# An encoder layer as a stream of weight tiles: one more buffer for classical tiles, seven products in one more projection block, and quarter sums of the residual made in another place

## The chip, the cores and the metric

The kernel runs on one core of a Trainium2 chip. The metric is the device time of one execution in microseconds (us), the median of several runs. Before the change it is 1144.56 us (three runs, 1144.2 to 1146.13).

The core's engines each run their own instruction stream: PE (matrix products; its weight loads are listed apart as PEld), DVE (vector), ACT (scalar, with its tables), POOL (GpSimd) and SP, which here only issues loads. Transfers run on 16 DMA engines that all queues of the core share. Products accumulate in eight PSUM banks of 128 x 512 floats.

## The reference

One layer of a transformer encoder on 256 positions of 2048 features, in float32:

```
n     = rmsnorm(x)
q_a, k_a, v_a, q_r, k_r, v_r, g_r = split(n @ W_in)      # 2048 x 7168
A     = attention of 8 heads (three dilated windows, ALiBi), softmax
R     = retention of 8 heads in both directions, normed per head, times silu(g_r)
h     = x + concat(A, R) @ W_out                          # 2048 x 2048
y     = rmsnorm(h + (silu(rmsnorm(h) @ W_gate) * (rmsnorm(h) @ W_up)) @ W_down)   # 5632 wide
```

Nearly all of the work is in the weight products, and the weights (some 220 MB) are read once.

## The kernel before, in words

**Precision.** A float32 product is made of three products of a shorter format: high by high, low by high, high by low. So each operand exists as a pair of halves. `halved` (L164) makes them: ACT copies the high half (its instructions carry L156, the line of the helper `copy`), then DVE subtracts it from the source for the low half (L159, the helper `tt`). A weight tile of 128 x 1024 floats (512 KB) thus costs one load on SP's queue, one ACT and one DVE instruction before PE can use it. In the profile the loaded tile is `rawc_...`, `raw_...` or `rawt_...`, its halves `ws_...`, the products' banks `p_...`.

**Blocks.** The weights are worked off in blocks of 1024 output columns in two sections: seven of the input projection (in0 to in6; pairs of q, k, v, g sections), two of the output projection (o0, o1), then three groups of gate-and-up blocks (gu0 to gu10) each followed by two down blocks. `ORDERS` writes the order of each block's steps out by hand. A step C is a classical weight tile: 12 matmuls into four banks. The steps 1a to 7a (and 1b to 7b) are the seven products of a Winograd scheme that replaces four classical tiles: 6 matmuls each, 42 in place of 48. Products 1, 2 and 4 read the activations themselves, 3, 5, 6 and 7 read quarter sums of them (`sa`), which `pair_sums` makes: four small DVE sums, then a halving. The weight side needs three or four loaded tiles, a sum on DVE into a tile `rawt`, another DVE sum and two accumulating DMAs on GpSimd's queue (`plus`, L176). The letters among the steps are hooks: M takes four banks of the seven products out and combines them (`mid`), H, T, N and K, Z do what belongs to the block before: scaling, transpositions and so on.

At the block's end its four remaining banks are taken out: `end_scaled` (four ACT copies with the row's norm factor) in a classical block of the input projection, `end_share` (four DVE adds to what `mid` left) in one with seven products, `end_out` in o0 and o1 (four DVE adds to the residual `ht`).

**Order and buffers.** The program is written out by one loop at the end over all steps. Before a step is issued, the weight tiles of the three steps after it (`AHEAD`) are prepared. Deferred work stands in lists: `soon` (run with the next step) and `later` (one entry popped after each step with a weight tile). Each engine executes in the order written; a wait on one engine delays what stands behind it there. Loads have their own order on SP's queue, by a scheduler, and each waits there until its buffer is free. The buffers of loaded tiles are the homes: three for tiles of C steps and of product 1 (`"c": 3`), three and two for further weight tiles of the seven products (`22`, `12`), one for their sum (`t`); retention uses free ones of `12`, `22` and `t` for its q, k and decay tiles meanwhile. Small tiles of 128 x 512 floats come from a pool of eight (`tmp`), the activations' halves from `actp`, of 24.

**Places that matter here.** In in4, in5 and in6 all tiles are classical. The last tile of such a block is run bank by bank, so that the banks' ends don't come all at once. In o1 the residual of the first half is transposed (`turn_n2(0)`, `turn_n2(1)`; `pt_n` on PE), scaled by the norm's weights and halved into `n2`, and its quarter sums are made from the same scaled copy `o_n`. The other half, `turn_n2(2)` and `turn_n2(3)`, is transposed in gu0, written to `n2` directly (DVE's L162 is the helper `stt`) and gets no sums, since gu0 has only one set of seven products. The later gate-and-up blocks have two (a over the first half of the 16 weight tiles, b over the second). `gate` (L717, called by the H hook of the next block) forms silu(gate) times up from gu0's parts by two ACT and two DVE instructions; then `turn_h` transposes the result on PE (`pt_h`).

Of the kernel before, what the change touches and what calls it, by code (L numbers as in the profile page):

```python
# [9 lines left out]
F32 = mybir.dt.float32  # L10
F32R = mybir.dt.float32r
AF = mybir.ActivationFunctionType
ALU = mybir.AluOpType
# [4 lines left out]
S = 256  # L18
# [4 lines left out]
KT = D // P  # L23
# [3 lines left out]
GROUPS = ((0, 4, 4), (4, 8, 4), (8, 11, 2))  # L27

INPUT = (((0, 0), (1, 0)), ((2, 0), (2, 1)), ((0, 1), (1, 1)), ((3, 0), (4, 0)), ((5, 0), (6, 0)), ((3, 1), (4, 1)), ((5, 1), (6, 1)))
KIND_IN = ("in0", "in1", "in", "in_c", "in_c", "in_c", "in_c")  # L30
AHEAD = 3
MAIN = "1a 5a H 2a C T 3a C 6a C 7a 1b C 4a 5b C 2b 6b C 7b M C C 3b 4b"
ORDERS = {
# [7 lines left out]
    "main": MAIN,  # L41
    "short": "1a 5a H 2a C T 3a C 6a C 7a C M C 4a C C C",
    "final": "1a 5a 2a C 3a C 6a C 7a M C 4a K K K K Z",
# [45 lines left out]
def encoder_layer(ctx: ExitStack, tc: tile.TileContext, xT, x, gains, gain_f, decay, tab, bias, w_st, y):  # L89
# [10 lines left out]
    wsp = ctx.enter_context(tc.tile_pool(name="wsp", bufs=5))  # L100
    actp = ctx.enter_context(tc.tile_pool(name="actp", bufs=24))
    resp = ctx.enter_context(tc.tile_pool(name="resp", bufs=4))
    tmp = ctx.enter_context(tc.tile_pool(name="tmp", bufs=8))
    psm = ctx.enter_context(tc.tile_pool(name="banks", bufs=8, space=bass.MemoryType.PSUM))
    flat = "p f t -> p (f t)"
    homes = {"c": 3, "22": 3, "12": 2, "t": 1}

    def atile(name, home=None, dtype=F32R):

# [4 lines left out]
    def ttile(name):  # L114
        return tmp.tile([P, 2, S], F32, tag="tmp", name=name)
# [10 lines left out]
    nw = const.tile([P, 2 * KT + NH], F32, name="nw")  # L126
# [8 lines left out]
    r1 = const.tile([P, 2], F32, name="r1")  # L135
    r2 = const.tile([P, 2], F32, name="r2")
    facs = const.tile([P, 2], F32, name="facs")
    sums_x, sums_h, sums_y = (const.tile([P, 2, 4], F32, name=f"sums_{n}") for n in "xhy")
# [4 lines left out]
    queue, later, soon, slots, stream = {}, [], [], ([], []), []  # L143

    def ch(ins):

        ins = ins.ins
        if ins.engine in queue:
            tc.add_manual_dep(
                ins, queue[ins.engine].name,  # L150
                mybir.DependencyInfo(mybir.DependencyClass.NoSync, mybir.DependencyReason.DATA), reason="stream",
            )
        queue[ins.engine] = ins
# [4 lines left out]
    def tt(out, x, y, op):  # L158
        ch(nc.vector.tensor_tensor(out, x, y, op=op))  # L159
# [4 lines left out]
    def halved(to, src):  # L164

        copy(to[:, :, 0, :], src)
        tt(to[:, :, 1, :], src, to[:, :, 0, :].bitcast(F32), ALU.subtract)
# [13 lines left out]
    def pair_sums(t, name):  # L181

        s = ttile(f"s_{name}")
        a11, a21, a12, a22 = (t[:, f, i * P:(i + 1) * P] for f in range(2) for i in range(2))
        s5, s2, s3, s4 = (s[:, f, i * P:(i + 1) * P] for f in range(2) for i in range(2))
        a = atile(f"sa_{name}")

        def add():
            for out, p, q, op in ((s5, a22, a21, ALU.subtract), (s2, a11, s5, ALU.add),
                                  (s3, a11, a21, ALU.subtract), (s4, a12, s2, ALU.subtract)):  # L190
                tt(out, p, q, op)

        later.extend([add, lambda: halved(a, s)])
        return a

    def square(out, src, func=AF.Square, **kw):
        copy(out, src, func, **kw)
# [171 lines left out]
    def turn(t, name, dst, w=None, sums=None, home=None):  # L369

        for p in range(2):
            pt = turned(t, p, name)
            a = atile(f"{name}_{p}", home)
            c = len(dst)
            dst.append(a)
            if sums is None:
                soon.append(lambda a=a, pt=pt, c=c: halved(a, pt) if w is None else weighed(a, pt, w[:, 2 * c:2 * c + 2]))
                continue
            o = ttile(f"o_{name}{p}")

            def take(a=a, pt=pt, c=c, o=o):
                if w is None:
                    copy(o, pt)
                else:
                    for f in range(2):
                        copy(o[:, f], pt[:, f], scale=w[:, 2 * c + f:2 * c + f + 1])
                halved(a, o)

            soon.append(take)
            sums.append(pair_sums(o, f"{name}_{p}"))  # L390
# [20 lines left out]
        tt(block.share[i, n], bank, block.share[i, n], ALU.add)  # L411


    xt, n1, n1_sums = {}, [], []

    def fetch_x(p):
        xt[p] = ttile(f"x_{p}")
# [2 lines left out]
    def part_x(p, f):  # L420
# [2 lines left out]
            n1.append(atile(f"n1_{p}"))  # L423
        copy(n1[p][:, f, 0], xt[p][:, f], scale=w)
        stt(n1[p][:, f, 1], xt[p][:, f], w, n1[p][:, f, 0].bitcast(F32), ALU.mult, ALU.subtract)

    def sums_n1():
        for p in range(2):
            t = ttile(f"xw_{p}")

            def weigh(p=p, t=t):
                tt(t, n1[p][:, :, 0].bitcast(F32), n1[p][:, :, 1].bitcast(F32), ALU.add)

            later.append(weigh)
            n1_sums.append(pair_sums(t, f"n1_{p}"))

    def measure_x():

# [207 lines left out]
    def many(*steps):  # L646
        def run():
            for step, *args in steps:
                step(*args)
        return run  # L650

    prev = None
    for b, sections in enumerate(INPUT + ((None, None),)):
        hooks = {}
        if b == 0:
            fetch_x(0)
            hooks = {"N": [sums_n1, measure_x]}
        else:
            (sec, half), _ = INPUT[b - 1]
            if sec in (0, 3):  # L660
                q, k = (q_a, k_a) if sec == 0 else (q_r, k_r)
                more = {1: [], 3: [(side_by_side, 0, 5, attention(2), attention(3))],
                        4: [(load_tables,), (side_by_side, 1, 3, retention_scores(0), retention_scores(1))],
                        6: [(side_by_side, 1, 3, retention_scores(2), retention_scores(3))]}[b]
                hooks = {"H": [many(*([(factor, r1, sums_x)] if b == 1 else []), *([(scaled, prev, 0, 1)] if sec == 0 else []))],
                         "T": [many((turn, lambda i, c=prev: c.share[i, 0], f"q{b}", q, None, None, "12" if sec else None)),
                               many((turn, lambda i, c=prev: c.share[i, 1], f"k{b}", k, None, None, "22" if sec else None), *more)]}
            elif sec == 2:
                hooks = {"H": [many((later.append, lambda c=prev: values(c, 0, v_a, 0)),
                                    (later.append, lambda c=prev: values(c, 1, v_a, 1)),  # L670
                                    (side_by_side, 0, 5, attention(0), attention(1)))]}
            else:
                hooks = {"H": [many()],
                         "T": [many((gates, prev, half), (side_by_side, 1, 1, retention_mix(2 * half), retention_mix(2 * half + 1)))]}
        if sections[0] is not None:
            prev = Block(f"in{b}", KIND_IN[b], n1, n1_sums, end_take if b == 0 else end_share if b < 3 else end_scaled, hooks,
                         opens=b == 0, early=b < 3)
            (sec, prev.half), _ = sections
            prev.values = sec == 5
# [3 lines left out]
    ht = []  # L683
    n2, n2_sums = [], []
# [17 lines left out]
            later.append(lambda: factor(r2, sums_h))  # L702

    def turn_n2(j):
        turn(lambda i: ht[j][:, i], f"n2_{j}", n2, nw[:, KT:2 * KT], n2_sums if j < 2 else None)

    for nb in range(2):
        if nb == 0:
            hooks = dict(into_out)
            hooks["H"] = [many((hooks["H"][0],), (load_residual, 0, 1))]  # L710
        else:
            hooks = {"T": [many((turn_n2, 0), (load_residual, 2, 3)), many((turn_n2, 1))]}
        b = Block(f"o{nb}", f"out{nb}", mixed, mixed_sums, end_out, hooks, parts="mid")
# [45 lines left out]
    for g, (lo, hi, s) in enumerate(GROUPS):  # L759
        h2, s2 = [], []  # L760
        hooks = {}
        for fb, kind in zip(range(lo, hi), kinds_gu()[g]):
            if fb == 0:
                hooks = {"T": [lambda: turn_n2(2), lambda: turn_n2(3)]}
            b = Block(f"gu{fb}", kind, n2, n2_sums, end_share, hooks)

            def turn_h(b=b, h2=h2, s2=s2, keep=2 * (fb - lo) < s, fb=fb):
                turn(lambda i: b.share[i, 0], f"h2_{fb}", h2, sums=s2 if keep else None)

            hooks = {"H": [lambda b=b: gate(b)], "T": [turn_h]}  # L770
        last = g == len(GROUPS) - 1
        for nb, kind in enumerate(kinds_dn()[g]):
            if last and nb == 0:
                hooks["H"] = [lambda h=hooks["H"][0]: (h(), load_gain())]
            b = Block(f"d{g}_{nb}", kind, h2, s2, end_dn, hooks, "mid" if last else "end")
            b.q, b.last, b.ended = 2 * nb, last, 0
            hooks = {}
# [4 lines left out]
    for i, (b, what, m) in enumerate(stream):  # L782
        done += i in work
        for k in work[:done + AHEAD]:
            if k >= i and k not in ready:
                c, w, n = stream[k]
# [90 lines left out]
```

## Time and profile before

| | |
|---|---|
| median of three runs | 1144.56 us (1144.2 to 1146.13) |
| profiled execution | 1142.88 us, its span 1140.8 us |
| mean granted clock of PE | 0.998 |
| PE busy | 1124.2 us, 5166 instructions |
| DVE busy | 923.4 us, 1056 instructions |
| ACT busy | 682.9 us, 841 instructions |
| POOL busy | 107.4 us, 135 instructions |
| read from HBM | 223.9 MB, 198 GB/s over the span |

The span runs from the first to the last instruction; the execution's own time is 2.1 us longer. In a timeline a row's columns are start, duration, engine, line, operation, output and inputs, count, and in brackets how long the engine had been idle before and which engine and instruction ended that. Rows of the waits give what waited for what, the sum in us, the times, and the longest. Rows of the chain are start, duration, what. In a table by stretches each engine has its busy time and count, and the last three columns are the clock, the busy share of the 16 DMA engines and GB/s. In rows of one tile's forms the three figures are the shortest, median and longest duration in ns. Matmul rows show the pipelined duration of the whole group; start to start is the pace.

### The profile page before, as it was taken

To read this page: it belongs to the slowest core of one execution; us is meant where nothing else is said; L and a number is where in the kernel's file an instruction comes from. 1 tells how busy PE (TensorE), PEld (TensorE's weight loads), DVE (VectorE), ACT (ScalarE), POOL (GpSimd) and SP (SyncE) were. 2 spreads that over 40 slices of the span, in tenths; PEclk is the share of its full clock that TensorE was granted. 3 is DMA by queue.
4 is the path that set the end of the run, shared out by engine and by line. 5 is a ranking of instruction groups with operands and counts; after the bars stand their busy time and mean duration, and the time that the engine had idled before them with its cause. 6 is when DMAs were issued, how large, how long until landed. Compare 5 with 4: busy or idle time off the path is not lost.

```text
span 1140.8 us, 14435 instructions
## 1 busy us (share of the span) xinstructions
PE 1124.2 (99%) x5166; PEld 933.2 (82%) x5166; DVE 923.4 (81%) x1056; ACT 682.9 (60%) x841; POOL 107.4 (9%) x135
## 2 busy tenths in 40 slices
PE   9999999999999998999999999999999999999996
PEld 7888888888888887788888887888888888888885
DVE  6668875855576777899989877999989977998985
ACT  6575665754656455666666654666666555666653
POOL 0102000000001110000000022000001102000011
PEclk9999999999999999999999999999999999999999
DMA  8969654465578686688897899998898899989885
GB/s 278 298 199 303 226 160 143 155 200 188 176 267 243 194 245 203 221 223 249 265 258 236 256 284 255 277 278 227 249 291 239 227 322 267 274 261 275 249 230 148
DMA packets 78535, 272.03 MB, mean 238 GB/s; under 512 B 9088, under 2 KB 9088, under 8 KB 78464
## 3 DMA queue, kind: packets, MB, share of 16 engines
q1 hardware_dynamic: 61776, 220.76, 55.7%
q0 software_dynamic: 15968, 49.29, 23.3%
q10 hardware_dynamic: 720, 1.07, 0.3%
q8 instruction: 40, 0.66, 0.2%
q14 instruction: 31, 0.25, 0.1%
HBM read 223.90 MB, written 2.10 MB: 198 GB/s over the span
## 4 chain that ended last, share of the span: by engine, by line
PE 76%; DMA 10%; DVE 8%; ACT 3%; issue 2%; POOL 0%; SPq 0%; DVEq 0%; ACTq 0%; POOLq 0%
PE p_gu L234 37%; PE p_d L234 17%; PE p_in L234 17%; DMA rawc_in<-in_w_st 5%; DMA rawc_o<-in_w_st 2%; DVE ws_in L159 2%; DMA rawc_gu<-in_w_st 2%; DVE ws_o L159 1%; PE p_o L234 1%; DVE ws_gu L159 1%; ACT ws_in L156 1%; PE pt_h L366 1%; DVE ws_d L159 1%; DVE ht L159 1%; DMA xs<-in_x 1%
## 5 line engine op out<-in xcount | busy, mean ns | idle before, releaser
L234 PE MATMUL p_gu<-ws_gu,n 128*128 128x512 f32 x1482 | 351.5, 390 | 5.0 <-DVE ht L159 3.1
L234 PEld LDWEIGHTS p_gu<-ws_gu,n 128*128 128x128 f32 x1482 | 277.7, 188 | 64.1 <-ACT ws_gu L156 5.3
L234 PE MATMUL p_in<-ws_in,n 128*128 128x512 f32 x1284 | 302.3, 392 | 1.3 <-ACT ws_in L156 1.3
L234 PEld LDWEIGHTS p_in<-ws_in,n 128*128 128x128 f32 x1284 | 238.3, 188 | 51.0 <-ACT ws_in L156 3.2
L159 DVE TENSOR_TENSOR ws_in<-rawc_in,ws_in 128x1024 fp32r<-128x1024 f32 (+1 forms) x107 | 129.0, 1212 | 63.0 <-ACT ws_in L156 62.3
L234 PE MATMUL p_d<-ws_d,h 128*128 128x512 f32 x708 | 167.7, 389 | 0.0
L159 DVE TENSOR_TENSOR ws_gu<-rawc_gu,ws_gu 128x1024 fp32r<-128x1024 f32 x113 | 137.7, 1220 | 27.4 <-ACT ws_gu L156 25.7
L234 PEld LDWEIGHTS p_d<-ws_d,h 128*128 128x128 f32 x708 | 132.7, 188 | 28.0 <-ACT ws_d L156 0.5
L156 ACT ACTIVATE ws_gu<-rawc_gu 128x1024 fp32r<-128x1024 f32 x113 | 118.7, 1055 | 59.2 <-PE p_gu L234 30.8
L156 ACT ACTIVATE ws_in<-rawc_in 128x1024 fp32r<-128x1024 f32 (+1 forms) x107 | 111.7, 1049 | 70.6 <-PE p_in L234 35.5
L234 PE MATMUL p_gu<-ws_gu,sa_n 128*128 128x512 f32 x504 | 128.5, 391 | 0.0
L234 PEld LDWEIGHTS p_gu<-ws_gu,sa_n 128*128 128x128 f32 x504 | 94.0, 188 | 19.1
L159 DVE TENSOR_TENSOR ws_gu<-raw_gu,ws_gu 128x1024 fp32r<-128x1024 f32 x84 | 102.4, 1219 | 2.4 <-ACT ws_gu L156 1.2
L156 ACT ACTIVATE ws_gu<-raw_gu 128x1024 fp32r<-128x1024 f32 x84 | 88.6, 1055 | 23.6 <-PE p_gu L234 20.4
L159 DVE TENSOR_TENSOR ws_d<-rawc_d,ws_d 128x1024 fp32r<-128x1024 f32 x54 | 65.8, 1221 | 18.1 <-ACT ws_d L156 17.5
L156 ACT ACTIVATE ws_d<-rawc_d 128x1024 fp32r<-128x1024 f32 x54 | 57.1, 1058 | 38.2 <-PE p_d L234 22.2
L156 ACT ACTIVATE ws_gu<-rawt_gu 128x1024 fp32r<-128x1024 f32 x42 | 44.4, 1056 | 57.0 <-DVE rawt_gu L159 37.3
L234 PE MATMUL p_d<-ws_d,sa_h 128*128 128x512 f32 x240 | 61.2, 390 | 0.0
L159 DVE TENSOR_TENSOR ws_gu<-rawt_gu,ws_gu 128x1024 fp32r<-128x1024 f32 x42 | 51.2, 1220 | 5.2 <-ACT ws_gu L156 5.1
L234 PEld LDWEIGHTS p_d<-ws_d,sa_h 128*128 128x128 f32 x240 | 44.8, 188 | 9.2
L156 ACT ACTIVATE ws_d<-raw_d 128x1024 fp32r<-128x1024 f32 x40 | 42.2, 1056 | 12.1 <-PE p_d L234 10.4
L159 DVE TENSOR_TENSOR ws_d<-raw_d,ws_d 128x1024 fp32r<-128x1024 f32 x40 | 48.8, 1219 | 0.5
(186 smaller groups left out, 1137.5 us busy)
## 6 DMA issues: line engine op xcount, KB each, us to landing
rawc_gu<-in_w_st SPq DMA_DIRECT2D x113, 512.0 KB, 5.1
rawc_in<-in_w_st SPq DMA_DIRECT2D x105, 512.0 KB, 4.1
raw_gu<-in_w_st SPq DMA_DIRECT2D x63, 512.0 KB, 5.4
rawc_d<-in_w_st SPq DMA_DIRECT2D x58, 512.0 KB, 5.1
raw_d<-in_w_st SPq DMA_DIRECT2D x30, 512.0 KB, 4.9
rawc_o<-in_w_st SPq DMA_DIRECT2D x26, 512.0 KB, 5.4
raw_gu<-raw_gu POOLq DMA_DIRECT2D x21, 512.0 KB, 6.8
raw_gu<-rawt_gu POOLq DMA_DIRECT2D x21, 512.0 KB, 5.3
```

The costliest lines, as they stand in the source:

```text
L156: ch(nc.scalar.activation(out, src, func, **kw))
L159: ch(nc.vector.tensor_tensor(out, x, y, op=op))
L234: ch(nc.tensor.matmul(self.bank(r), x[u], w[v], start=r not in self.begun, stop=self.left[r] == 0))
L366: ch(nc.tensor.transpose(pt[:, f, i * P:(i + 1) * P], t(i)[:, (2 * p + f) * P:(2 * p + f + 1) * P], ident))
```

## The change

There are three parts.

1. The homes for classical tiles go from three to four, the small tiles from eight to seven. The size of `rawp` grows by 4 KB of each partition and that of `tmp` falls by 2 KB.
2. in5 changes from classical tiles to the kind that has one set of seven products and twelve classical tiles. Its quarter sums are made a second time, in in4, by a new hook S behind ten classical tiles: `sums_of` adds the halves of each of the first two activation tiles back together (`whole`) and calls `pair_sums`. in5's end becomes `end_share`, and the norm's factor is applied in in6's H hook by four ACT copies (`scaled`).
3. In o1 `turn_n2(1)` makes no sums. Its two tiles of `n2` are written directly from PSUM. A hook S in gu0, behind M, makes these sums through `sums_of` from `n2`.

`sums_of` also replaces `sums_n1` (the same steps) for the first blocks.

```diff
-KIND_IN = ("in0", "in1", "in", "in_c", "in_c", "in_c", "in_c")
+KIND_IN = ("in0", "in1", "in", "in_c", "in_c", "in", "in_c")
...
-    "in_c": "C H C T C T C C C C C C C C C C C C C",
+    "in_c": "C H C T C T C C C C C C C S C C C C C C",
...
-    "gu_first": "C 1a 5a C 2a T C C C T C 3a 6a C 7a C 4a M C C C C",
+    "gu_first": "C 1a 5a C 2a T C C C T C 3a 6a C 7a C 4a M S C C C C",
...
-    tmp = ctx.enter_context(tc.tile_pool(name="tmp", bufs=8))
+    tmp = ctx.enter_context(tc.tile_pool(name="tmp", bufs=7))
...
-    homes = {"c": 3, "22": 3, "12": 2, "t": 1}
+    homes = {"c": 4, "22": 3, "12": 2, "t": 1}
...
+    def sums_of(parts, pairs, to):
+
+        for p in pairs:
+            t = ttile(f"whole{p}")
+
+            def whole(p=p, t=t):
+                tt(t, parts[p][:, :, 0].bitcast(F32), parts[p][:, :, 1].bitcast(F32), ALU.add)
+
+            later.append(whole)
+            to.append(pair_sums(t, f"again{p}"))
...
-                hooks = {"H": [many(*([(factor, r1, sums_x)] if b == 1 else []), *([(scaled, prev, 0, 1)] if sec == 0 else []))],
+                hooks = {"H": [many(*([(factor, r1, sums_x)] if b == 1 else []), *([(scaled, prev, 0, 1)] if sec == 0 or half else []))],
...
-            prev = Block(f"in{b}", KIND_IN[b], n1, n1_sums, end_take if b == 0 else end_share if b < 3 else end_scaled, hooks,
+            if b == 4:
+                hooks["S"] = [many((sums_of, n1, range(2), n1_again))]
+            end = end_take if b == 0 else end_share if "1a" in ORDERS[KIND_IN[b]] else end_scaled
+            prev = Block(f"in{b}", KIND_IN[b], n1, n1_again if b > 2 else n1_sums, end, hooks,
...
-        turn(lambda i: ht[j][:, i], f"n2_{j}", n2, nw[:, KT:2 * KT], n2_sums if j < 2 else None)
+        turn(lambda i: ht[j][:, i], f"n2_{j}", n2, nw[:, KT:2 * KT], n2_sums if j == 0 else None)
...
-                hooks = {"T": [lambda: turn_n2(2), lambda: turn_n2(3)]}
+                hooks = {"T": [lambda: turn_n2(2), lambda: turn_n2(3)], "S": [lambda: sums_of(n2, range(2, 4), n2_sums)]}
```

How the instructions move shows in their order, at two places on DVE and one on SP. In the names of these rows the block follows the tile's kind: `ws_gu0` is a weight tile's halves in gu0, `ht2` a part of the residual, `p2_o1` a bank of o1, and the last number counts the tiles.

DVE, from the last weight tiles of o1 to the residual adds that empty o1's banks; `s_n2_1_0` are small sums, `sa_n2_1_0` the low half of the quarter sums. Before:

```order
L159 TENSOR_TENSOR n2_1_1_3565<-o_n2_11_3566,n2_1_1_3565 128x2x256
L159 TENSOR_TENSOR s_n2_1_0_3558<-o_n2_10_3557 128x128
L159 TENSOR_TENSOR s_n2_1_0_3558<-o_n2_10_3557,s_n2_1_0_3558 128x128
L159 TENSOR_TENSOR s_n2_1_0_3558<-o_n2_10_3557 128x128
L159 TENSOR_TENSOR s_n2_1_0_3558<-o_n2_10_3557,s_n2_1_0_3558 128x128
L159 TENSOR_TENSOR ws_o1_3600<-rawc_o1_3598,ws_o1_3600 128x2x512
L159 TENSOR_TENSOR sa_n2_1_0_3559<-s_n2_1_0_3558,sa_n2_1_0_3559 128x2x256
L159 TENSOR_TENSOR ws_gu0_3619<-rawc_gu0_3617,ws_gu0_3619 128x2x512
...
L159 TENSOR_TENSOR sa_n2_1_1_3568<-s_n2_1_1_3567,sa_n2_1_1_3568 128x2x256
L159 TENSOR_TENSOR ws_gu0_3664<-rawt_gu0_3647,ws_gu0_3664 128x2x512
L159 TENSOR_TENSOR rawt_gu0_3647<-rawt_gu0_3647,raw22_gu0_3642 128x1024
L159 TENSOR_TENSOR ht2_3397<-p2_o1_3296,ht2_3397 128x512
```

And now:

```order
L159 TENSOR_TENSOR ws_o1_3607<-rawc_o1_3605,ws_o1_3607 128x2x512
L162 SCALAR_TENSOR_TENSOR n2_1_0_3598<-pt_n2_10_3593,nw_78,n2_1_0_3598 128x256 x2
L162 SCALAR_TENSOR_TENSOR n2_1_1_3604<-pt_n2_11_3599,nw_78,n2_1_1_3604 128x256 x2
L159 TENSOR_TENSOR ws_o1_3632<-rawc_o1_3630,ws_o1_3632 128x2x512
L159 TENSOR_TENSOR ws_gu0_3649<-rawc_gu0_3647,ws_gu0_3649 128x2x512
L159 TENSOR_TENSOR ws_gu0_3670<-rawc_gu0_3664,ws_gu0_3670 128x2x512
L159 TENSOR_TENSOR rawt_gu0_3673<-rawc_gu0_3664,raw12_gu0_3666 128x1024
L159 TENSOR_TENSOR ws_gu0_3688<-rawt_gu0_3673,ws_gu0_3688 128x2x512
L159 TENSOR_TENSOR rawt_gu0_3673<-rawt_gu0_3673,raw22_gu0_3668 128x1024
L159 TENSOR_TENSOR ht2_3439<-p2_o1_3338,ht2_3439 128x512
```

Eight small sums and two low halves have left the stretch ahead of the residual adds.

DVE, from gu0's end to its gate (the two rows with `r2`). Before:

```order
L159 TENSOR_TENSOR part1_gu0_3950<-p4_gu0_3695,part1_gu0_3950 128x512
L159 TENSOR_TENSOR part3_gu0_3952<-p8_gu0_3698,part3_gu0_3952 128x512
L159 TENSOR_TENSOR ws_gu1_4040<-rawc_gu1_4038,ws_gu1_4040 128x2x512
L159 TENSOR_TENSOR ws_gu1_4050<-raw22_gu1_3980,ws_gu1_4050 128x2x512
L162 SCALAR_TENSOR_TENSOR part0_gu0_3949<-part2_gu0_3951,r2_91,part0_gu0_3949 128x512
L162 SCALAR_TENSOR_TENSOR part1_gu0_3950<-part3_gu0_3952,r2_91,part1_gu0_3950 128x512
```

And now:

```order
L159 TENSOR_TENSOR part3_gu0_3976<-p8_gu0_3722,part3_gu0_3976 128x512
L159 TENSOR_TENSOR whole3_3986<-n2_1_1_3604 128x512
L159 TENSOR_TENSOR ws_gu1_4078<-rawc_gu1_4076,ws_gu1_4078 128x2x512
L159 TENSOR_TENSOR s_again3_3987<-whole3_3986 128x128
L159 TENSOR_TENSOR s_again3_3987<-whole3_3986,s_again3_3987 128x128
L159 TENSOR_TENSOR s_again3_3987<-whole3_3986 128x128
L159 TENSOR_TENSOR s_again3_3987<-whole3_3986,s_again3_3987 128x128
L159 TENSOR_TENSOR ws_gu1_4092<-raw22_gu1_4011,ws_gu1_4092 128x2x512
L159 TENSOR_TENSOR sa_again3_3988<-s_again3_3987,sa_again3_3988 128x2x256
L162 SCALAR_TENSOR_TENSOR part0_gu0_3973<-part2_gu0_3975,r2_91,part0_gu0_3973 128x512
L162 SCALAR_TENSOR_TENSOR part1_gu0_3974<-part3_gu0_3976,r2_91,part1_gu0_3974 128x512
```

The second whole, its small sums and its low half stand between gu0's end and its gate; the first whole and its sums stand in the same way a little ahead of that end, among the last weight tiles.

SP, from the end of d0_1 to the first tiles of gu4; `rawc` is a classical home, `raw12` and `raw22` are the others. Before:

```order
L253 DMA raw12_gu4_5664<-in_w_st 128x1024
L253 DMA rawc_d0_1_5574<-in_w_st 128x1024
L253 DMA rawc_d0_1_5600<-in_w_st 128x1024
L253 DMA raw22_gu4_5666<-in_w_st 128x1024
L253 DMA rawc_d0_1_5611<-in_w_st 128x1024
L253 DMA rawc_gu4_5662<-in_w_st 128x1024
L253 DMA raw12_gu4_5796<-in_w_st 128x1024
L253 DMA rawc_gu4_5716<-in_w_st 128x1024
L253 DMA rawc_gu4_5738<-in_w_st 128x1024
L253 DMA raw22_gu4_5699<-in_w_st 128x1024
```

And now:

```order
L264 DMA rawc_d0_1_5618<-in_w_st 128x1024
L264 DMA raw12_gu4_5708<-in_w_st 128x1024
L264 DMA rawc_d0_1_5644<-in_w_st 128x1024
L264 DMA rawc_d0_1_5655<-in_w_st 128x1024
L264 DMA raw22_gu4_5710<-in_w_st 128x1024
L264 DMA rawc_gu4_5706<-in_w_st 128x1024
L264 DMA rawc_gu4_5760<-in_w_st 128x1024
L264 DMA raw12_gu4_5840<-in_w_st 128x1024
L264 DMA rawc_gu4_5782<-in_w_st 128x1024
L264 DMA rawc_gu4_5812<-in_w_st 128x1024
```

The classical loads have each moved one place forward, past the loads for the other homes beside them.

More of the change, by code (lines that the diff above doesn't have):

```diff
@@ L411, in end_share @@
         tt(block.share[i, n], bank, block.share[i, n], ALU.add)
-    xt, n1, n1_sums = {}, [], []
+    xt, n1, n1_sums, n1_again = {}, [], [], []
     def fetch_x(p):
@@ L425, in part_x @@
         stt(n1[p][:, f, 1], xt[p][:, f], w, n1[p][:, f, 0].bitcast(F32), ALU.mult, ALU.subtract)
[L427 to L435, printed above, removed]
     def measure_x():
@@ L656, in encoder_layer @@
             fetch_x(0)
-            hooks = {"N": [sums_n1, measure_x]}
+            hooks = {"N": [many((sums_of, n1, range(2), n1_sums)), measure_x]}
         else:
```

## The prediction

> **What bounds the kernel now.** I read the page first, then the waits of the matrix engine, then the chain of waits, and last the timelines of PE, DVE and ACT around each wait. The page and the waits:
>
> ```profile
> PE 1124.2 (99%) x5166; PEld 933.2 (82%) x5166; DVE 923.4 (81%) x1056; ACT 682.9 (60%) x841; POOL 107.4 (9%) x135
> PE p_gu L234 <- DVE ht L159: 3.1, 1, 3.1
> PE p_in L234 <- ACT ws_in L156: 1.3, 2, 0.7
> PE p_gu L234 <- ACT ws_gu L156: 1.1, 1, 1.1
> PE p_gu L234 <- DVE n L162: 0.8, 1, 0.8
> ```
>
> PE is busy 99% of 1140.8 us; time can leave only as matmuls or as one of these few waits. The pace of a matmul is not its mean duration, which contains pipelining; it comes from an unbroken stretch of the chain:
>
> ```profile
> 494.28 40.82 PE p_gu L234 x180
> ```
>
> 40.82 / 180 = 0.2268 us each, so a Winograd product (6 matmuls) takes 1.36 and a classical tile (12) 2.72. With that pace the places where PE stopped can be sized as start to start in its timeline:
>
> ```profile
> 52.75 4.24 PE L234 MATMUL p_in<-ws_in,n 128*128 128x512 f32 x18
> 57.65 3.06 PE L234 MATMUL p_in<-ws_in,n 128*128 128x512 f32 x12 [0.66 <-ACT ws_in L156]
> ...
> 437.88 2.88 PE L234 MATMUL p_gu<-ws_gu,n 128*128 128x512 f32 x12
> 443.90 1.62 PE L234 MATMUL p_gu<-ws_gu,n 128*128 128x512 f32 x6 [3.14 <-DVE ht L159]
> ...
> 451.60 6.05 PE L234 MATMUL p_gu<-ws_gu,n 128*128 128x512 f32 x25
> 458.44 2.79 PE L234 MATMUL p_gu<-ws_gu,n 128*128 128x512 f32 x11 [0.80 <-DVE n L162]
> ...
> 710.43 1.52 PE L234 MATMUL p_gu<-ws_gu,n 128*128 128x512 f32 x6
> 713.03 3.24 PE L234 MATMUL p_gu<-ws_gu,n 128*128 128x512 f32 x13 [1.08 <-ACT ws_gu L156]
> ```
>
> Each next row should start at the earlier start plus count times 0.2268. At 52.75 + 18 x 0.2268 = 56.83 the next came 0.82 late; at 437.88 + 2.72 = 440.60, 3.30 late; at 451.60 + 25 x 0.2268 = 457.27, 1.17 late; at 710.43 + 1.36 = 711.79, 1.24 late. Together 6.5 us: all that the waits can give. The chain and ACT tell what stood behind them:
>
> ```profile
> 427.90 1.06 ACT L156 ACTIVATE ws_o<-rawc_o 128x1024 fp32r<-128x1024 f32 x1 [3.93 <-DMA rawc_o<-in_w_st]
> 448.98 6.59 DMA rawc_gu<-in_w_st
> 700.95 10.87 DMA rawc_gu<-in_w_st
> 48.95 6.95 DMA xs<-in_x
> ```
>
> The second and third are loads into the classical home that PE ended up waiting for (457 and 711). The first is such a load late in o1; DVE falls behind after it, and 440 follows. The fourth is no weight load.
>
> **The change part by part.** *Seven products in in5.* Six matmuls fewer: -6 x 0.2268 = -1.36 us. DVE gets 29 instructions more, ACT 4, GpSimd two accumulating DMAs. Where they fall (in4, in5 and the start of in6), the windows show room:
>
> ```profile
> core 0: us, PE busy (x) PEld busy (x) DVE busy (x) ACT busy (x) POOL busy (x), PEclk, DMA share, GB/s
> 44.00:57.00 13.00, 12.99 (x58) 10.42 (x56) 7.17 (x6) 8.26 (x15) 3.65 (x7) 1.00 0.99 321
> 240.00:300.00 60.00, 60.00 (x293) 50.42 (x292) 28.89 (x32) 30.81 (x37) 2.05 (x2) 1.00 0.55 182
> 441.00:457.00 16.00, 13.10 (x62) 10.89 (x62) 10.51 (x12) 7.87 (x14) 0.87 (x1) 1.00 0.81 223
> 460.00:660.00 200.00, 200.00 (x904) 166.05 (x903) 185.31 (x205) 125.38 (x138) 20.47 (x23) 1.00 0.83 244
> 688.00:701.00 13.00, 13.00 (x59) 10.78 (x58) 12.96 (x15) 7.10 (x7) 4.64 (x6) 1.00 0.79 204
> 701.00:712.00 11.00, 10.95 (x49) 8.73 (x47) 5.69 (x5) 2.21 (x3) 1.48 (x2) 1.00 1.06 272
> ```
>
> In 240 to 300 DVE and ACT are busy 29 and 31 of 60 us and the DMA engines 0.55, so nearly all is covered. Uncovered would be the sums of the second pair, which 5a, in5's second product, needs. They come at the very end of in4, where ACT has its four end copies to make:
>
> ```profile
> 244.86 0.69 ACT L156 ACTIVATE v_in<-p_in,r 128x512 fp32r<-128x512 f32 x1 [2.34 <-PE p_in L234]
> 246.90 0.69 ACT L156 ACTIVATE part_in<-p_in,r 128x512 f32<-128x512 f32 x1
> ...
> L159 DVE TENSOR_TENSOR xw<-n x2: 683/684/684, 23.6 to 31.7; 128x512 f32<-128x512 f32 x2
> L159 DVE TENSOR_TENSOR s_n<-xw x4: 284/284/286, 25.7 to 34.4; 128x128 f32<-128x128 f32 x4
> L156 ACT ACTIVATE sa_n<-s_n x6: 612/632/634, 27.1 to 437.2; 128x512 fp32r<-128x512 f32 x6
> L159 DVE TENSOR_TENSOR sa_n<-s_n,sa_n x6: 683/684/691, 28.4 to 439.4; 128x512 fp32r<-128x512 f32 x6
> ```
>
> in4's last tile runs bank by bank, 3 matmuls (0.68) each; the first bank's copy starts at 244.86, so PE ends the last near 244.7 + 3 x 0.68 = 246.7. Product 1a carries PE to 248.1; 5a's fourth matmul, at 248.1 + 3 x 0.2268 = 248.7, wants the low half of the second sums. That is 246.90 + 0.69 + 0.63 (ACT, high half) + 0.68 (DVE, low half) = 248.9 and a release. I take +0.3, bounds 0 (the high half slips in before the last copy) and +0.5.
>
> *Sums of the residual out of o1.* These DVE rows stand ahead of the residual adds that free the bank awaited at 440.60:
>
> ```profile
> 432.38 0.29 DVE L159 TENSOR_TENSOR s_n<-o_n 128x128 f32<-128x128 f32 x1
> ...
> 433.32 1.22 DVE L159 TENSOR_TENSOR ws_o<-rawc_o,ws_o 128x1024 fp32r<-128x1024 f32 x1
> 434.45 0.68 DVE L159 TENSOR_TENSOR sa_n<-s_n,sa_n 128x512 fp32r<-128x512 f32 x1
> 435.05 1.23 DVE L159 TENSOR_TENSOR ws_gu<-rawc_gu,ws_gu 128x1024 fp32r<-128x1024 f32 x1
> ...
> 443.07 2.48 DVE L159 TENSOR_TENSOR ht<-p_o,ht 128x512 f32<-128x512 f32 x4
> ```
>
> Four small sums cost 433.32 - 432.38 = 0.94, a low half 435.05 - 434.45 = 0.60; both come twice: 3.08 us. The adds then start at 440.0, the first is out near 440.7, and PE's stall of 3.30 shrinks to 0.2 to 0.3 by this alone (-3.0). If the fourth home also brings o1's loads earlier, everything on DVE starts sooner and all of it goes: **-3.30** (bounds -2.4, if the 0.60 of one low half turns into a wait for ACT, and -3.30). What comes next behind it is the wait of 457, below.
>
> *The same sums in gu0 and gu1.* They now need a whole again (0.60 at pace), four small sums (0.94) and a low half (0.60), twice: 4.3 us; by whole durations 2 x (0.68 + 4 x 0.285 + 0.68) = 5.0. They stand ahead of the gate of gu0, which pt_h on PE needs, and first themselves for gu1's 5b, later still. DVE has little room (185 of 200 us busy in 460 to 660), but here are two gaps:
>
> ```profile
> 478.52 1.23 DVE L159 TENSOR_TENSOR ws_gu<-rawc_gu,ws_gu 128x1024 fp32r<-128x1024 f32 x1 [0.38 <-ACT ws_gu L156]
> ...
> 482.09 1.23 DVE L159 TENSOR_TENSOR ws_gu<-rawt_gu,ws_gu 128x1024 fp32r<-128x1024 f32 x1 [1.21 <-ACT ws_gu L156]
> ...
> 490.29 1.41 DVE L162 SCALAR_TENSOR_TENSOR part_gu<-part_gu,r,part_gu 128x512 f32<-128x512 f32 x2
> ...
> 493.25 1.03 PE L366 MATMUL pt_h<-ident,part_gu 128*128 128x128 f32 x8
> ```
>
> The first whole and its four sums (0.60 + 0.94 = 1.54) fill 0.38 + 1.21 = 1.59. The rest, 0.60 + 0.60 + 0.94 + 0.60 = 2.74, pushes the gate, which ended at 490.29 + 1.41 = 491.70, to 494.44. PE's second transposition reads it at about 493.4, so there PE stops for **+1.0**; bounds 0 (DVE reaches gu0 earlier once the waits ahead are gone) and +1.6 (nothing fits the smaller gap).
>
> *A fourth classical home.* SP's queue issues each classical load one place earlier, a tile's time (2.72) or more sooner where a free home was what it waited for. 457 was 1.17 late behind a load of 6.59 and 711 was 1.24 late behind one of 10.87: one step is enough for either if the load then runs at its own speed. I take **-1.17** and **-1.24**; bounds 0 (no bandwidth to spare) and the whole. For 711 the stretch before it, 688 to 701, had a DMA share of 0.79, so a load could start in it. For 457 the share is 0.81. At 57 nothing is taken: the share is 0.99, and ACT was held by a square whose data came on GpSimd's queue; bounds -0.82 and +0.5, should an earlier weight load delay that data.
>
> The Trainium skill, "DMA: Bandwidth & Descriptors", section "Queues, rings and completion order", says that each DMA engine takes turns, packet by packet, between the queue rows for which it has work. By that rule a load issued earlier into full engines takes its share from its neighbours and nothing is won; at 44 to 57 (0.99) the trace is in such a state, at 688 to 701 (0.79) it is not. With the rule in force at 457 and 711 as well the sum would be R1's.
>
> *The small tile less* (8 to 7) has one use that now waits closely, the square of a retention head in in5, with three prepared tiles in front of PE; cost 0.
>
> Sum: -1.36 - 3.30 - 1.17 - 1.24 + 0.3 + 1.0 = -5.77. The profiled execution took 1142.88 us around its span of 1140.8, 1.7 under the median of the runs; the sum applied to it gives 1137.1, and to the median, which is what is compared, 1144.56 - 5.77 = **1138.8**. By the bounds with the home at work, 1136.7 (-1.36 - 3.30 - 1.17 - 1.24 - 0.82) to 1141.
>
> **The rivals.** R1, the home buys nothing: the loads at 457 and 711 are slow because the engines are full (701 to 712: 1.06), and one place earlier only moves the queue. Then -1.36 - 3.0 + 0.3 + 1.0 = -3.1: 1141.5. Against it speak the shares of 0.79 and 0.81 ahead of both.
>
> R2, the moved sums find no gap in gu0: the 5.0 us less the slack of the gate (493.4 - 491.7 = 1.7) stop PE for 3.3, and the home buys nothing: -1.36 - 3.0 + 0.3 + 3.3 = -0.8: 1143.8. For it speaks DVE's 93% in 460 to 660, against it the two gaps above.
>
> R3, slower: DVE is the limit from o1 on. The load that ended at 427.90, not the sums, sets when DVE reaches the residual adds, so the 3.30 stays (and 457 and 711 with it), while all 5.0 of the moved sums come out on PE between gu1 and gu2, where DVE never catches up: -1.36 + 0.3 + 5.0 = +3.9: 1148.5. It turns slower than can be told from no change once more than 3.4 us of the sums reach PE with the waits unchanged. Against it: in the rows above DVE goes from 432.38 to 435.05 without a break, sums in between, so what is taken out there does bring the adds forward.
>
> That the change doesn't do what it says is excluded by the order of the changed program: the loads do stand one place earlier in SP's queue, and in5 has six matmuls fewer.
>
> **How the numbers follow.** My forecast 0.62, R1 0.22, R2 0.10, R3 0.04, 0.02 for anything else. A measurement of this kernel tells about 0.2%, 2.3 us, from no change, so faster begins below 1142.3. Forecast and R1 lie there: 0.84; R2 and the rest lie within: 0.11; R3 and a little of the unknown beyond: 0.05. The range holds the forecast's bounds and R1 with its costs at their top (-1.36 - 3.0 + 0.5 + 1.6 = -2.3: 1142.3), less 0.4 below for the scatter of the runs: 1136.3 to 1142.4.
>
> **What would show it.** In the profile after: PE without "<- DVE ht" at gu0's 1a, the adds starting at 440 less 1.4 or before; no "<- DVE n" and no "<- ACT ws_gu" at what was 457 and 711, and shorter DMA pieces in the chain there; a new wait of PE on part_gu at the first pt_h of about 1.0, and one on sa in in5 of 0.3. It is wrong if the waits for late loads stay in place (R1), if the pt_h wait is 3 us or more (R2), or if PE waits for ws_gu on DVE all through gu1 and gu2 with the ht wait still there (R3).

## The result and the profile after

| | before | after |
|---|---|---|
| median of five runs | 1144.56 us (1143.55 to 1147.38) | 1134.68 us (1134.37 to 1135.35) |
| profiled execution, its span | 1142.88, 1140.8 | 1134.37, 1132.4 |
| mean granted clock in it | 0.998 | 0.998 |

The ratio is 0.9913 (95% interval 0.9897 to 0.993): 9.9 us faster where 5.8 were forecast, and under the range's lower end of 1136.3. The scatter of the runs fell too, from 3.8 to 1.0 us. A few executions of the experiments below lie far outside the scatter of their kernel (one at 1252 us, the others above 2300); all medians, spans and ratios leave them out.

The page of the changed kernel has this chain by engine, where before 10% of the span was DMA; and PE has two waits left, that of the start (which was there before) and one at gu0's gate:

```profile
PE 96%; DVE 2%; issue 1%; DMA 0%; ACT 0%; SPq 0%; DVEq 0%; POOLq 0%; POOL 0%; ACTq 0%
...
PE p_in L794 <- POOL zero L125: 1.3, 1, 1.3
PE pt_h L377 <- DVE part_gu L162: 0.3, 1, 0.3
```

In PE's timeline of the changed kernel, each place can be sized as in the prediction, start to start at 0.2268 us a matmul:

```profile
52.23 6.96 PE L245 MATMUL p_in<-ws_in,n 128*128 128x512 f32 x30
...
115.22 2.88 PE L245 MATMUL p_in<-ws_in,n 128*128 128x512 f32 x12
117.94 0.88 PE L484 MATMUL ps_sa<-k,q 128*128 128x256 f32 x6
...
245.98 1.79 PE L245 MATMUL p_in<-ws_in,sa_again 128*128 128x512 f32 x6
247.61 4.71 PE L245 MATMUL p_in<-ws_in,n 128*128 128x512 f32 x20
...
434.79 4.55 PE L245 MATMUL p_gu<-ws_gu,n 128*128 128x512 f32 x18
439.19 1.54 PE L245 MATMUL p_gu<-ws_gu,sa_n 128*128 128x512 f32 x6
...
445.44 8.42 PE L245 MATMUL p_gu<-ws_gu,n 128*128 128x512 f32 x36
...
481.79 4.24 PE L245 MATMUL p_gu<-ws_gu,n 128*128 128x512 f32 x18
486.11 0.33 PE L377 MATMUL pt_h<-ident,part_gu 128*128 128x128 f32 x1
486.77 0.98 PE L377 MATMUL pt_h<-ident,part_gu 128*128 128x128 f32 x7 [0.33 <-DVE part_gu L162]
487.51 1.62 PE L245 MATMUL p_gu<-ws_gu,sa_n 128*128 128x512 f32 x6
...
703.81 5.60 PE L245 MATMUL p_gu<-ws_gu,n 128*128 128x512 f32 x24
```

The wait at 57 is gone (30 matmuls without a break). So is one that the prediction did not count: the first attention scores `ps_sa` start at 115.22 + 12 x 0.2268 = 117.94, on time. Before, their row was 0.43 late:

```profile
116.73 2.88 PE L234 MATMUL p_in<-ws_in,n 128*128 128x512 f32 x12
119.88 0.98 PE L483 MATMUL ps_sa<-k,q 128*128 128x256 f32 x6 [0.27 <-ACT part_in L156]
```

in5's 5a takes 247.61 - 245.98 = 1.63 in place of 1.36, so 0.27 late. The eighteen matmuls from 434.79 end 0.32 late where the sum had 3.30 before. The one at 457 lies inside the unbroken 36, the one at 711 inside the unbroken 24. What is lost is at gu0's gate: pt_h should start at 481.79 + 18 x 0.2268 = 485.87 and take 0.79 (494.04 - 493.25 before); the product behind it starts at 487.51, 0.85 late.

Why the load that ended at 711 is no longer late is seen in SP's timeline, first of before. gu4's first three classical loads have gone out from 680.16 to 684.8; here are the fourth and fifth, then the sixth, the first of the pair at 700.95:

```profile
691.57 7.44 SPq L253 DMA_DIRECT2D rawc_gu<-in_w_st  x2
...
700.95 2.60 SPq L253 DMA_DIRECT2D rawc_gu<-in_w_st  x2
```

In the changed kernel the second of gu4 goes out at 671.05; here are the third and fourth, then the fifth and sixth:

```profile
675.08 1.69 SPq L264 DMA_DIRECT2D rawc_gu<-in_w_st  x2
...
684.29 7.58 SPq L264 DMA_DIRECT2D rawc_gu<-in_w_st  x2
```

The sixth leaves at 684.29 + 7.58 - 0.33 = 691.5. PE is 694.11 - 687.49 = 6.6 us ahead at gu4's first product, so in the times of before that is 698.1: 2.8 us earlier, and the wait had been 1.24. By the views of the DMA it also took 6.7 us to landing in place of 10.9; why it was quicker isn't shown. The engines as a whole are as full there as they were (row of the stretches after, DMA share 1.04):

```profile
694.00:706.00 12.00, 12.00 (x54) 9.93 (x54) 10.09 (x9) 6.25 (x6) 1.36 (x2) 1.00 1.04 279
```

### The profile page after: what moved, and what is told of

Same layout as the page of the kernel before. It is cut to its first block, busy times and chain, and to the rows that moved or that the text cites. A ratio compares the mean times of both kernels' runs of the same rounds, so it can differ in the third digit from the quotient of the medians.

```text
span 1132.4 us, 14473 instructions
## 1 busy us (share of the span) xinstructions
PE 1121.7 (99%) x5160; PEld 932.5 (82%) x5160; DVE 942.5 (83%) x1085; ACT 690.8 (61%) x845; POOL 110.5 (10%) x137
## 4 chain that ended last, share of the span: by engine, by line
PE 96%; DVE 2%; issue 1%; DMA 0%; ACT 0%; SPq 0%; DVEq 0%; POOLq 0%; POOL 0%; ACTq 0%
PE p_gu L245 38%; PE p_in L245 26%; PE p_d L245 19%; PE p_o L245 7%; PE pt_h L377 1%; DVE ws_gu L159 1%; PE ps_or L495 1%; PE ps_oa L495 1%; PE ps_sa L484 1%; PE ps_sr L484 1%; DMA rawc_in<-in_w_st 0%; PE pt L529 0%; PE pt_n L377 0%; PE pt_q L377 0%; PE pt_k L377 0%
## 5 line engine op out<-in xcount | busy, mean ns | idle before, releaser
L245 PE MATMUL p_in<-ws_in,n 128*128 128x512 f32 x1254 | 295.4, 391 | 0.2
L245 PEld LDWEIGHTS p_in<-ws_in,n 128*128 128x128 f32 x1254 | 232.8, 188 | 48.3 <-ACT ws_in L156 1.6
L159 DVE TENSOR_TENSOR ws_in<-rawc_in,ws_in 128x1024 fp32r<-128x1024 f32 (+1 forms) x104 | 125.5, 1212 | 42.3 <-ACT ws_in L156 41.8
L156 ACT ACTIVATE ws_in<-rawc_in 128x1024 fp32r<-128x1024 f32 (+1 forms) x104 | 108.4, 1049 | 44.7 <-PE p_in L245 34.3
L245 PE MATMUL p_gu<-ws_gu,sa_n 128*128 128x512 f32 x264 | 67.6, 392 | 0.0
L245 PE MATMUL p_gu<-ws_gu,sa_again 128*128 128x512 f32 x240 | 60.9, 389 | 0.0
L159 DVE TENSOR_TENSOR ws_gu<-rawt_gu,ws_gu 128x1024 fp32r<-128x1024 f32 x42 | 51.3, 1221 | 9.3 <-ACT ws_gu L156 9.3
L245 PEld LDWEIGHTS p_gu<-ws_gu,sa_n 128*128 128x128 f32 x264 | 49.0, 188 | 9.8
L245 PEld LDWEIGHTS p_gu<-ws_gu,sa_again 128*128 128x128 f32 x240 | 45.0, 188 | 9.4
```

The costliest lines, as they stand in the source:

```text
L156: ch(nc.scalar.activation(out, src, func, **kw))
L245: ch(nc.tensor.matmul(self.bank(r), x[u], w[v], start=r not in self.begun, stop=self.left[r] == 0))
```

## The experiments

The theory behind the record (S below) is that each part removes its own waits. Its rival, formed on seeing the profile after (H), is that a full classical home makes loads late everywhere, also the load behind DVE's lateness in o1, so that the home does nearly all. Each ratio compares with runs of the kernel before on the same occasion; their medians were 1144.15 us for e1 to e4 (29 runs), 1144.06 for e10 to e12 (11) and 1144.43 for e7, e13 and e14 (16). Differences between kernels of different occasions are less sure than these ratios.

**e1_home_alone.** The kernel before, with

```diff
-    tmp = ctx.enter_context(tc.tile_pool(name="tmp", bufs=8))
+    tmp = ctx.enter_context(tc.tile_pool(name="tmp", bufs=7))
-    homes = {"c": 3, "22": 3, "12": 2, "t": 1}
+    homes = {"c": 4, "22": 3, "12": 2, "t": 1}
```

> The kernel before with the fourth home and seven small tiles, nothing else. Theory H (a full home is what makes loads late everywhere, also those behind DVE's lateness in o1): the waits at 57, 457 and 711 go and the one at 440 shrinks to under 1, in all 0.9 + 1.2 + 1.3 + 2.5 to 3.3 and 0.4 at the first attention scores: 6 to 7 us faster than before, 1138, and the runs scatter by about 1 us in place of 4. Theory S (each part has its own wait, as in the prediction): only 457 and 711 go, 2.4 faster, 1142, and the ht wait at 440 stays at 3 us.

Measured: 1134.91 us (1134.7 to 1136.22), ratio 0.9921 (0.9908 to 0.9934). Two small changes of buffers give 9.2 of the 9.9 us. No ht wait is left in the waits of this kernel: besides that of the start they list 0.2 us on a first weight tile. Its timelines show why. These are DVE's row and the chain's load of before for the late tile of o1 (DVE before that idled 3.76 us for it):

```profile
428.99 1.23 DVE L159 TENSOR_TENSOR ws_o<-rawc_o,ws_o 128x1024 fp32r<-128x1024 f32 x1 [3.76 <-ACT ws_o L156]
...
420.55 7.24 DMA rawc_o<-in_w_st
```

And these are rows of SP, DVE and PE with the home:

```profile
414.90 3.98 SPq L253 DMA_DIRECT2D rawc_o<-in_w_st  x2
...
422.41 1.23 DVE L159 TENSOR_TENSOR ws_o<-rawc_o,ws_o 128x1024 fp32r<-128x1024 f32 x1 [1.61 <-ACT ws_o L156]
...
428.51 0.68 DVE L159 TENSOR_TENSOR sa_n<-s_n,sa_n 128x512 fp32r<-128x512 f32 x1
429.99 1.23 DVE L159 TENSOR_TENSOR ws_gu<-rawc_gu,ws_gu 128x1024 fp32r<-128x1024 f32 x1 [0.80 <-ACT ws_gu L156]
...
438.01 2.48 DVE L159 TENSOR_TENSOR ht<-p_o,ht 128x512 f32<-128x512 f32 x4
...
436.06 4.40 PE L234 MATMUL p_gu<-ws_gu,n 128*128 128x512 f32 x18
440.30 1.54 PE L234 MATMUL p_gu<-ws_gu,sa_n 128*128 128x512 f32 x6
```

The sums still stand ahead of the adds. But the load of o1's late tile goes out at 414.90 where before it went out at 420.55, when its home came free, and the tile is halved at 422.41 where before it was 428.99. PE is 437.88 - 436.06 = 1.8 us ahead, so the load is 3.8 us and DVE 4.8 us earlier against PE, and DVE even idles between. The adds start at 438.01, and 1a, due at 436.06 + 2.72 = 438.78, is 0.16 late (18 matmuls in 4.24 in place of 4.08).

**e2_sums_alone.** The changed kernel with three homes, eight small tiles and in5 classical, so only

```diff
-... n2_sums if j < 2 else None)
+... n2_sums if j == 0 else None)
-    "gu_first": "C 1a 5a C 2a T C C C T C 3a 6a C 7a C 4a M C C C C",
+    "gu_first": "C 1a 5a C 2a T C C C T C 3a 6a C 7a C 4a M S C C C C",
```

> The kernel before with only the sums of the residual's first half moved from o1 to gu0 (three homes, eight small tiles, in5 classical). Both theories: the ht wait at 440 shrinks from 3.3 to 0.3 and a wait of 0.8 for the gate appears at the first pt_h: 2.2 us faster, 1142.3, with the waits at 57, 457 and 711 still there. If instead the load before the sums sets 440 (the third rival), the wait at 440 stays at 3 and the time is 0.8 over before or more.

Measured: 1142.70 us (1140.63 to 1146.16), ratio 0.999 (0.9977 to 1.0003). Two of its waits:

```profile
PE pt_h L377 <- DVE part_gu L162: 0.8, 2, 0.4
PE p_gu L245 <- DVE ht L159: 0.6, 1, 0.6
```

The ht wait goes from 3.1 to 0.6 (start to start from 3.30 to 0.72, where the prediction had 0.2 to 0.3): the sums are a cause of the wait too. Either cause taken away alone closes most of it, so the two gains don't add. What this part gave in time can't be told from nothing.

**e3_in5_alone.** The kernel before with in5's kind `"in"` and its sums in in4.

> The kernel before with only the seven products in in5 and their sums in in4. Both theories: six matmuls fewer, 1.36, less a wait of 0.3 for the low half of the second sums: 1.1 us faster, 1143.5; the waits at 57, 440, 457 and 711 stay. If with three homes its further loads come late, waits of PE in in5 show it and the time is that of before or over it.

Measured: 1143.04 us (1140.72 to 1146.08), ratio 0.999 (0.998 to 1.000): of the size expected, but hardly to be told from nothing. Its profile showed something else, in PE's timeline behind the ht wait:

```profile
437.73 2.88 PE L245 MATMUL p_gu<-ws_gu,n 128*128 128x512 f32 x12
443.43 2.27 PE L245 MATMUL p_gu<-ws_gu,n 128*128 128x512 f32 x6 [2.81 <-DVE ht L159]
445.50 2.51 PE L245 MATMUL p_gu<-ws_gu,sa_n 128*128 128x512 f32 x6
447.84 4.27 PE L245 MATMUL p_gu<-ws_gu,n 128*128 128x512 f32 x18
```

Two products take 447.84 - 443.43 = 4.41 in place of 2.72; the granted clock over 440 to 448 was 0.79. The wait cost 2.98 itself and 1.7 more behind it. In the profiled execution of before the same wait was followed by nearly full pace (446.72 - 443.90 = 2.82).

**e4_no_home.** The changed kernel with `"c": 3` and eight small tiles.

> The changed kernel with three homes and eight small tiles again. Theory H: with the sums and in5 left, 2.2 + 1.1 = 3.3 us faster than before, 1141.2, with waits at 57, 457 and 711 back and a scatter as before; so the home is worth 6 of the change's 9.9. Theory S: 440 gone by the sums, 457 and 711 back: 9.9 less 2.4, so 7.5 faster, 1137.

Measured: 1142.65 us (1140.03 to 1145.33), ratio 0.9986 (0.9975 to 0.9998). 1.6 us are left without the home, against 7.5 by theory S and 3.3 by H. S falls. H's own size is missed too: 3.3 lies outside the interval (0.2 to 2.9), and the waits at 57, 457 and 711 are joined by 1.3 at pt_h. So the sums and in5 were worth little without the home, and the home some 8 us with them.

**e10_home_in5.** The changed kernel with the sums back in o1 (e2's lines undone).

> The changed kernel with the residual's sums back in o1: the fourth home and the seven products in in5 alone. If the home alone already closes the wait at 440, the moved sums only cost (0.8 at the first pt_h in the changed kernel): 1134.9 of the home alone less 1.1 for in5, 1133.8, and no wait at pt_h. If the moved sums are still needed once in5 is shorter, the ht wait comes back and it is 1135 or slower.

Measured: 1133.86 us (four runs, 1133.11 to 1134.35), ratio 0.9912 (0.9897 to 0.9927). All four lie under the lowest of the changed kernel (1134.37), by 0.8 in the middle; but these runs were made on another occasion, and the ratios to before, 0.9912 and 0.9913, don't tell the two kernels apart. The profiles do. This one's only wait is that of the start, and its PE rows at gu0's start and behind pt_h are:

```profile
435.19 4.24 PE L245 MATMUL p_gu<-ws_gu,n 128*128 128x512 f32 x18
439.27 1.52 PE L245 MATMUL p_gu<-ws_gu,sa_n 128*128 128x512 f32 x6
...
486.73 1.62 PE L245 MATMUL p_gu<-ws_gu,sa_n 128*128 128x512 f32 x6
```

The eighteen matmuls end on time with the sums in o1 (4.08), and the way to the product behind pt_h takes 486.73 - 435.19 = 51.54 us, where the changed kernel took 487.51 - 434.79 = 52.72: with the home at work, moving the sums costs 1.2 us there, 0.85 of it at pt_h and 0.32 at 440.

**e11_home_stall.** e1 with the wait at 440 made again:

```diff
+        if block.q and not block.squares:
+            slow = ttile("slow").rearrange(flat)
+            for _ in range(5):
+                tt(slow, o, o, ALU.add)
         tt(o, bank, o, ALU.add)
```

> The kernel of the home alone with five additions of 0.60 us put on DVE ahead of o1's residual adds (into a small tile that nothing reads), so that the wait of the kernel before at 440 is made again and nothing else. If a wait costs what it lasts: 1134.9 + 3.0 = 1137.9, the runs as close together as without it. If PE's clock also falls behind such a wait, as the profile of in5 alone shows (8 matmuls at 427 ns after the wait at 440), some runs cost up to 1.6 more: a median of 1138 to 1139.5, a scatter of 2 or more and a mean granted clock under 0.997.

**e13_short_stall.** The same with `range(2)`.

> The kernel of the home alone with two additions on DVE ahead of o1's residual adds in place of five: a wait at 440 of 1.2 in place of 2.9. If PE's clock falls behind a wait of any length: 1134.9 + 1.2 + 1.6 = 1137.7 in most runs. If only a long wait does it: 1136.1, clock 0.997 or 0.998, and the matmuls behind the wait at 227 ns.

Measured: five additions 1139.44 us (1137.47 to 1139.84), two 1136.02 (1134.93 to 1136.75). Rows of PE and of the stretches, of e11, then of e13:

```profile
436.76 2.88 PE L234 MATMUL p_gu<-ws_gu,n 128*128 128x512 f32 x12
442.40 2.08 PE L234 MATMUL p_gu<-ws_gu,n 128*128 128x512 f32 x6 [2.76 <-DVE ht L159]
444.28 2.70 PE L234 MATMUL p_gu<-ws_gu,sa_n 128*128 128x512 f32 x6
446.82 4.27 PE L234 MATMUL p_gu<-ws_gu,n 128*128 128x512 f32 x18
...
439.95:443.37 3.42, 0.97 (x4) 0.86 (x5) 3.25 (x6) 1.56 (x3) 0.00 (x0) 1.00 0.02 5
443.37:446.78 3.41, 3.41 (x9) 2.65 (x8) 3.41 (x5) 1.67 (x3) 0.17 (x1) 0.50 0.11 32
```

```profile
436.49 2.88 PE L234 MATMUL p_gu<-ws_gu,n 128*128 128x512 f32 x12
440.54 1.63 PE L234 MATMUL p_gu<-ws_gu,n 128*128 128x512 f32 x6 [1.16 <-ACT ws_gu L156]
...
438.00:446.00 8.00, 6.84 (x31) 5.37 (x30) 7.86 (x11) 4.92 (x9) 0.87 (x1) 1.00 0.44 114
```

The long wait is 442.40 - 439.48 = 2.92, and the two products behind it take 4.42 in place of 2.72: 2.92 + 1.70 = 4.62, against 1139.44 - 1134.91 = 4.5 measured. In one of its six runs the mean clock was 0.998 in place of 0.996, and that one came out at 1137.47, 2.6 over e1: the wait alone. The short wait, 440.54 - 439.21 = 1.33, left the clock at 1.00, and costs 1.1. (Its row names ACT, but the first residual add ended at 440.33, and PE starts 0.2 behind that, as in e11.) So here a wait near 3 us is paid one and a half times in most runs, a single one near 1 us once.

The Trainium skill, "TensorE: Matmul & The Clock Gate", Part 1, says that PE's clock is halved behind an idle window of about 3.4 us and comes back after as long a busy one, and that the window runs free. The traces agree on the length and on the free run: the granted clock of e11 is 0.50 for just one stretch of 3.41 us, and from the clock's rise at 6.46 to its fall at 443.37 there are 436.9 us, 128 times 3.413; from 446.78 to the next fall, at 1132.86, there are 686.1, 201 times. So the changes lie on a grid that takes no notice of when a wait begins. They differ on how much idle time is enough: a window need not be idle throughout. In the one before the fall PE had no matmul for 442.40 - 439.95 = 2.45 us, in e3 for 443.43 - 440.76 = 2.67.

This also tells why the profiled run of before kept its pace. Its wait lasted from 440.60 to 443.90, and its grid, carried back from the fall at 1135.47, has an edge at 442.56: 1.96 us without a matmul in one window, 1.34 in the next, and the clock stayed at 1.00 in both. That the one run of e11 with a clock of 0.998 had its wait split in this way is likely, but its trace isn't kept.

**e7_seven_small_alone.** The kernel before with the small tiles alone cut to seven.

> The kernel before with seven small tiles and three homes. The prediction put the small tile at nothing: 1144.1 as before, within 0.7. If the tile is worth something, it is slower, and the home's own worth is larger than the 9.2 measured for both.

Measured: ratio 1.0002 (0.9988 to 1.0016). The small tile is worth nothing that can be told from the scatter (1.8 us at most), so e1's gain is the home's.

**e14_home_from_22.** The kernel before with the fourth home taken from the kind 22.

```diff
-    homes = {"c": 3, "22": 3, "12": 2, "t": 1}
+    homes = {"c": 4, "22": 2, "12": 2, "t": 1}
```

> The kernel before with four classical homes and two of the kind 22 in place of three and three: the same memory, eight small tiles. If what counts is the place of the classical loads in the queue, most of the home's gain comes back: 1135 to 1138. If the 22 loads were just as near to late, waits for raw_gu and raw_d come in place of those for rawc: 1141 or more.

Measured: 1171.37 us, ratio 1.0234 (1.0215 to 1.0252). The waits moved to where no long one had been. Rows of PE's waits and of ACT's:

```profile
PE p_d L234 <- ACT ws_d L156: 6.7, 2, 3.6
PE p_gu L234 <- ACT ws_gu L156: 5.8, 4, 2.9
...
ACT ws_gu L156 <- DMA raw_gu<-in_w_st: 75.3, 18, 9.4
```

The first two are 12.5 us of the 27; its mean clock is 0.992. ACT now waits for loads into 22 homes (`raw_gu`), for which it didn't wait before. The classical home was the short one only while 22 had three.

**e12_in3_too.** A candidate on these findings: the home, seven products in in5 and in in3, the quarter sums of the first blocks kept for both instead of made again, the residual's sums in o1. Cut from its edit against the changed kernel:

```diff
-KIND_IN = ("in0", "in1", "in", "in_c", "in_c", "in", "in_c")
+KIND_IN = ("in0", "in1", "in", "in", "in_c", "in", "in_c")
...
-            prev = Block(f"in{b}", KIND_IN[b], n1, n1_again if b > 2 else n1_sums, end, hooks,
+            prev = Block(f"in{b}", KIND_IN[b], n1, n1_sums, end, hooks,
```

> A candidate: the fourth home, seven products in in5 and in in3 also, with the quarter sums of the first blocks kept for both in place of made again, and the residual's sums in o1. Two times 1.36 less two waits of up to 0.3: 1134.9 - 2.1 = 1132.8, if the loads of in3 find their homes while the attention runs; 1134 or more if they come late.

Measured: 1132.25 us (1131.8 to 1132.5), ratio 0.9898 (0.9884 to 0.9912): the fastest here, 2.7 under e1, which is what 2 x 1.36 gives.

## Why the prediction was wrong, point by point

- *Which step failed.* The terms that the sum counted came out in all as put. PE's start in the changed kernel against before, with the restart behind each wait, gives -1.0 in in5, -3.1 at 440, -1.2 at 457, -1.4 at 711 and +0.8 at pt_h: -5.8, as -5.77 was put. The miss of 4.1 us lies in what was put at nothing: 2.5 in the span (-1.0 at 57, -0.5 at the first attention scores, -0.5 at the start, -0.5 in small restarts) and 1.5 between span and median. That the sum of the terms came out is in part luck, since the cause of the largest was booked wrongly (sums out of o1, below).
- *What bounds the kernel.* Right: late classical loads and the bank at 440. The waits held 6.5 us by its list; it left out 0.43 at the first attention scores. The 0.5 at the start can't be booked to the change: the first product with quarter sums starts at 51.3 to 53.0 in the five profiles with three homes and at 50.9 to 51.8 in the seven with four.
- *In5.* -1.36 + 0.27, as put.
- *Sums out of o1, -3.30.* The size is right, the cause is not, and this is the step of the mechanism that failed. The wait had two causes that lie one behind the other on DVE, a late load and the sums, and the step gave all of it to the one that the diff touched. e2 shows that the sums nearly suffice (3.1 to 0.6), e1 that the load does as well. Given the home, moving the sums gains nothing.
- *Sums in gu0, +1.0.* Measured 0.85, at the place named. With the step above, the third part as a whole is a loss of some 1 us in the profiles.
- *The fourth home, -2.41.* Alone it is 9.2. Its two waits went, as put (1.17 and 1.24). It also took the 440 (3.1), which had been booked elsewhere, and the 57 (0.82). At 57 the reason for nothing was that ACT was held by a square whose data came on GpSimd's queue. That is so, but the data in turn stood behind a classical load, by the chain of before and, last, GpSimd's row after:

```profile
38.89 5.63 DMA rawc_in<-in_w_st
...
48.39 0.46 POOL raw_in L179
...
43.21 1.97 POOL L444 DMA_DIRECT2D xs<-in_x  x3
```

GpSimd sends the square's data right behind an accumulating DMA, which waits for DVE's sum of a tile from that load. Before, the data went out at 48.95, now at 43.21. The wait at 57 is in all five profiles with three homes and in none of the seven with four. The 0.43 at the attention scores is in three of the five and in none of the seven.
- *A wait costs what it lasts.* Assumed without saying, when the sum of one profiled execution was taken off the median. That execution had a clock of 0.998 and full pace behind its wait; it was one of the better runs. Over 29 runs of before the mean clock was 0.9962, and the time followed it: 1140.94 to 1144.06 at 0.998, 1145.86 and 1147.63 at 0.993. One stretch of 3.41 us at half clock takes 0.0015 off the mean clock of a run and costs 1.7 us; the mean of before lies 0.0014 under the changed kernel's 0.9976, so about one such stretch a run, an estimate of 1.6 us. The median's 9.9 is 1.5 more than the span's 8.4.
- *R1 (full DMA engines)* had it that an earlier place wins nothing at a share of 1.0. The stretch after is as full (1.04), and nothing waits: the load went out 2.8 us earlier. The rule of the Trainium skill ("DMA: Bandwidth & Descriptors", "Queues, rings and completion order") is about turns between queue rows; the weight loads all go out on SP's one queue, and when a load may begin the rule doesn't say. *R2* falls with the 0.85 at pt_h, where it had 3.3. *R3* was right that the late load sets when DVE reaches the adds (e1), and wrong that the sums don't (e2).

The span's 8.4 is thus -0.5 (start), -1.0 (57), -0.5 (attention scores), -1.0 (in5), -3.1 (440), -1.2 (457), +0.8 (pt_h), -1.4 (711) and -0.5 in small restarts; the median has 1.5 more by the clock.

## What to carry to other kernels

Where two delays stand one behind the other ahead of a wait, taking away either may end it: a gain is booked to a part only after asking what the other parts alone would do. A buffer that the loads wait for is looked for wherever a late load sets off a delay, also several steps before the engine that stops. And before a sum is made on one profiled execution, its clock and time are set beside those of all runs: a scatter of several us, as here, can mean that something in it is paid in some runs only.

## What was not expected of the hardware

A PE wait of 2.8 to 2.9 us was followed by 3.4 us at half pace in five of six runs; one of 1.3 was not. Waits that stand close together count together: in e7's profile two of about 1 us, with a single matmul between them, had the same slow stretch behind them, by its PE timeline and clock. They lie in one window of the clock's grid, 456.55 to 459.96, with some 2.1 us without a matmul:

```profile
458.54 0.50 PE L234 MATMUL p_gu<-ws_gu,n 128*128 128x512 f32 x1 [0.84 <-ACT n L156]
459.83 4.37 PE L234 MATMUL p_gu<-ws_gu,n 128*128 128x512 f32 x11 [0.79 <-DVE n L162]
464.04 1.04 PE L366 MATMUL pt_n<-ident,ht 128*128 128x128 f32 x8
...
459.96:463.38 3.42, 3.42 (x9) 2.68 (x10) 3.17 (x7) 3.07 (x5) 0.62 (x1) 0.50 0.42 153
```

Eleven matmuls take 464.04 - 459.83 = 4.21 in place of 2.49. So in these traces the clock fell behind a window of 3.41 us with about 2.1 us or more without a matmul, and not behind one with 1.96.
